# The last two token blocks of a decoder trunk, multiplied jointly by seven products instead of eight

## The chip, the cores and the metric

The kernel runs on one core of one Trainium2 chip. The metric is the device time of one execution in microseconds (us); a profiled execution also has a span, from its first to its last instruction. Engines: PE (TensorE, matmuls), DVE (VectorE), ACT (ScalarE), POOL (GpSimd), SP (SyncE, which issues the DMA transfers). SBUF is the on-chip memory, PSUM the memory that matmuls write (eight banks of 128 x 512 fp32).

## The reference

One layer over 2048 tokens of width 1024, in fp32:

```
h <- x + concat[ SSD(384) | RG-LRU(256) | FoX attention(384) ]( rms(x) W_in ) W_out
h <- h + ( silu(u W_gate) * (u W_up) ) W_down          u = rms(h) * g2, inner width 2816
h <- h + sigmoid( rms(h)*g3 W_pg + b ) * ( p W_pp )    p has width 256
out = rms(h) * gf
```

FoX is causal attention of 6 heads x 64, swept over queries. `W_out` and `W_pg` are 1024 x 1024.

## The kernel before

All activations lie transposed: 128 features on the partitions, tokens along the free axis. The tokens are cut into four blocks of 512 (`TB`, `NTB`), the width into 8 tiles of 128 (`KD`), the inner width into 22 (`NF`).

Every fp32 number is kept as two fp32r numbers, a rounded one and the rest. A weight block (128 output columns, 8 input tiles) comes by DMA into a staging tile (`wst`, 2 buffers), ACT writes its rounded half (L179) and POOL the rest (L180) into a tile `w` (3 buffers); that is `weight`. `parts` and `split` do the same for activations with ACT and DVE into the tiles `u0` to `u7` (2 buffers each). `mm3` (L190 to L192) then makes three matmuls of 128 x 128 by 128 x 512 for each input tile: high x high, high x low, low x high, 24 for a full output tile, into one of three PSUM banks `mm`. Five more banks (`xa` to `xe`) serve the rest.

The program has three phases, each with its own tile pools. Phase 1 projects and runs the RG-LRU; phase 1b runs the convolutions and the SSD and, beside them, attention of query chunk 0. Phase 3 (`phase3`) loops over the four token blocks `tb`: gate and up products in three groups of inner tiles (`FSPLIT`), each followed by its part of the down product added into `h`; then the norm g3, `W_pp`, `W_pg` and the final norm with the output. Attention of chunk `tb + 1` is a generator that runs beside the feed-forward part: `mm3` advances it by `rate / KD` pieces for each input tile (`Side.tick`), with `rate` = its number of pieces over `RATE`. `load_y` then reads back the heads' outputs (`dy`) of the next block, and `mix` makes its `W_out` product beside `W_pg`, so that the next block can start at once. Block 3 has neither attention nor a next block.

`rms` turns a sum of squares (`square_sum`, tiles `ssq` with 1 buffer and `sq` with 3) into reciprocal roots along the tokens: eight small matmuls (L135), a power on POOL (L139), and two matmuls that spread it over the partitions (L149).

The order on each engine is not the order of the code: the tile framework's scheduler lists instructions by readiness and by their place in the program, fixes each engine's queue when the program is built, hands out buffers and adds the semaphores. Each engine then executes its own queue in order.

Of the kernel before, what the change touches and what calls it, by code (L numbers as in the profile page):

```python
# [2 lines left out]

# [1 line left out]

# [6 lines left out]
F32 = mybir.dt.float32  # L12
F32R = mybir.dt.float32r
ACT = mybir.ActivationFunctionType
ALU = mybir.AluOpType
# [16 lines left out]
RATE = 45  # L32


PC = {}
# [29 lines left out]
class Trunk:  # L65
# [589 lines left out]
    def phase3(self, ctx):  # L655
        nc, tc, a = self.nc, self.tc, self.a
        pool = lambda name, bufs, **kw: ctx.enter_context(tc.tile_pool(name=name, bufs=bufs, **kw))
        one = pool("m4one", 1)
        two = pool("m4two", 2)
        V = nc.vector  # L660
        hbp = self.t(one, [P, 8], "hbp")
        nc.vector.tensor_scalar(hbp, self.pc("bple", 0, 8), 0.5, None, op0=ALU.mult)
        side = self.side

        h, u = self.first
        for tb in range(NTB):
            tsl = slice(tb * TB, (tb + 1) * TB)
            more = tb + 1 < NTB
            rate = 0
            if more:  # L670
                side.start(self.attention(tb + 1, one, ("xa", "xe", "xb", "xc"), "xd"))

                rate = 6 * (8 * (tb + 2) + 1) / RATE
            for f0, f1 in zip(FSPLIT[:-1], FSPLIT[1:]):
                hid = []
                for f in range(f0, f1):
                    pg = self.mm3(self.weight(a["w_gate"][f], KD), u, rate)
                    pu = self.mm3(self.weight(a["w_up"][f], KD), u, rate)
                    th = self.t(two, [P, TB], "th")
                    nc.scalar.activation(th, pg, ACT.Tanh, scale=0.5)  # L680
                    nc.vector.scalar_tensor_tensor(th, th, 1.0, pg, op0=ALU.add, op1=ALU.mult)  # L681
                    nc.vector.tensor_tensor(th, th, pu, op=ALU.mult)  # L682
                    hh = self.u(f - f0)
                    nc.scalar.activation(hh[:, 0], th, ACT.Copy, scale=0.5)  # L684
                    nc.vector.scalar_tensor_tensor(hh[:, 1], th, 0.5, hh[:, 0].bitcast(F32), op0=ALU.mult, op1=ALU.subtract)  # L685
                    hid.append(hh)
                if f1 == NF and more:
                    yx = self.load_y(tb + 1)
                for c in range(KD):
                    ps = self.mm3(self.weight(a["w_down"][c, :, f0:f1], f1 - f0), hid, rate)  # L690
                    nc.vector.tensor_tensor(h[c], h[c], ps, op=ALU.add)  # L691
            u = self.norm_split(h, "g3", eng=V, tag="xe")

            px = self.t(one, [P, 4, TB], "kx", F32R)
            px = [px[:, 0:2], px[:, 2:4]]
            for k in range(2):
                y = self.load(a["pt"][k, :, tsl])
# [12 lines left out]
            hn = []  # L710
            for c in range(KD):
                while more and len(hn) < min(c + 4, KD):
                    hn.append(self.mix(tb + 1, len(hn), yx))
# [6 lines left out]
                nc.vector.scalar_tensor_tensor(em[c], th, 0.5, h[c], op0=ALU.mult, op1=ALU.add)  # L720
            if more:
                h, u = hn, un
            rb = self.rms(self.square_sum(em, V), D, "xb")
            for k in range(KD):
                nc.vector.scalar_tensor_tensor(em[k], em[k], self.pc("gf", k), rb, op0=ALU.mult, op1=ALU.mult)
                nc.sync.dma_start(self.out[k, :, tsl], em[k])

    def build(self, phases=3):
        tc, nc = self.tc, self.nc
        with ExitStack() as ctx:  # L730
            pool = lambda name, bufs, **kw: ctx.enter_context(tc.tile_pool(name=name, bufs=bufs, **kw))
            self.cpool = pool("const", 1)
            self.small = pool("small", 2)
            self.tmp = pool("tmp", 2)
            self.dpool = pool("scratch", 1, space=DRAM)
            self.wst, self.wsp = pool("wst", 2), pool("w", 3)
            self.upool = pool("u", 2)
            self.pmm, self.px = pool("pmm", 3, space=PSUM), pool("px", 1, space=PSUM)
            for nm, shape in (("dq", [3, P, 2, T]), ("dk", [3, P, 2, T]), ("dv", [T // P, P, 6 * P]), ("dy", [KD, P, T]),
                              ("du", [NTB, KD, P, TB]), ("ddt", [NTB, P, 2, NCH, 6]),  # L740
                              ("drow", [NTB, NCH * 12, P]), ("dcum", [6, T])):
                setattr(self, nm, self.t(self.dpool, shape, nm))
            self.consts()
            for i, ph in enumerate((self.phase1, self.phase1b, self.phase3)):
                if i == 1:
                    self.hp = pool("h", KD + 3)
                if i < phases:
                    with ExitStack() as c2:
                        ph(c2)
# [50 lines left out]

# [10 lines left out]
```

## Time and profile before

| | us |
|---|---|
| median of 3 runs | 2932.22 (2927.58 to 2932.3) |
| the profiled execution, device time | 2928.33 |
| its span | 2926.6 |
| PE busy | 2812.5 |
| DVE busy | 1751.9 |
| POOL busy | 1213.2 |
| ACT busy | 1175.7 |

Busy time of PE counts pipelined matmuls whose ends are modelled: one of 128 x 512 shows as about 396 ns, while a new one starts every 0.23 us. In a row of groups the columns are line, engine, operation, output tile <- input tiles, shapes, count, then busy us and mean ns of one, then the engine's idle time just before them and what ended it. A row of stretches has start:end, length, and for each engine the busy time with the number of instructions, the granted clock, the share of DMA time and GB/s. A row of the timeline has start, duration, engine (q: issue only), line, operation, tiles, shapes, how many were merged, and in brackets the idle time before and what ended it. A row of one line's instructions has the shortest, median and longest duration in ns.

### The profile page before, as it was taken

The numbers are of one execution on the slowest core, as the hardware profiler recorded it, in microseconds if no ns is written. First come the engines' busy times: TensorE is split into PE (matmuls) and PEld (weight loads), VectorE is DVE, ScalarE is ACT, GpSimd is POOL, SyncE is SP. The second block draws the span as 40 slices with busy tenths as digits, with TensorE's granted clock in tenths as the row PEclk, the third lists the DMA queues.
The fourth block names the chain that finished last, engine by engine and source line by source line (L and its number), as shares of the span: only waits on it lengthen the run. The fifth ranks groups of instructions, "written<-read, shape, count | busy, mean of one in ns | idle before, by whom it ended". The sixth has DMA issues, their size and how long they took to land.

```text
span 2926.6 us, 35034 instructions
## 1 busy us (share of the span) xinstructions
PE 2812.5 (96%) x12981; PEld 2317.3 (79%) x12981; DVE 1751.9 (60%) x3001; ACT 1175.7 (40%) x1751; POOL 1213.2 (41%) x635
## 2 busy tenths in 40 slices
PE   6998999998999999999999999999999999999997
PEld 5777777777888888887888888788888887888885
DVE  7888768988754543637655446464665464523246
ACT  5555434444333332434444334344444343322233
POOL 5544445432443434443333334443333344444442
PEclk9999999998999999999999999999999999999998
DMA  5544544452354343434343334243443233332231
GB/s 181 172 164 159 162 142 141 132 162 80 136 157 131 119 122 104 142 123 133 118 147 104 127 105 146 100 146 115 133 122 114 91 130 108 116 97 92 100 100 65
DMA packets 156221, 368.60 MB, mean 126 GB/s; under 512 B 17644, under 2 KB 49036, under 8 KB 154508
## 3 DMA queue, kind: packets, MB, share of 16 engines
q1 hardware_dynamic: 156050, 366.36, 38.6%
q8 instruction: 103, 1.69, 0.2%
q14 instruction: 68, 0.56, 0.1%
HBM read 322.01 MB, written 44.29 MB: 125 GB/s over the span
## 4 chain that ended last, share of the span: by engine, by line
PE 72%; DVE 3%; issue 1%; DMA 1%; ACT 1%; POOL 0%; POOLq 0%; DVEq 0%; ACTq 0%
PE mm L191 20%; PE mm L192 20%; PE mm L190 20%; PE xd L609 2%; PE xd L608 2%; PE xa L603 1%; DMA ld<-dy 1%; PE xe L603 1%; PE xb L603 1%; PE xc L603 1%; PE xa L572 0%; PE xa L573 0%; DVE th L719 0%; DVE u L168 0%; PE xb L573 0%
## 5 line engine op out<-in xcount | busy, mean ns | idle before, releaser
L180 POOL TENSOR_TENSOR w<-wst,w 128x1024 fp32r<-128x1024 f32 (+1 forms) x424 | 1031.8, 2435 | 1365.6 <-ACT w L179 1300.5
L190 PE MATMUL mm<-u,w 128*128 128x512 f32 x3264 | 1295.9, 399 | 16.5 <-ACT u L200 8.9
L191 PE MATMUL mm<-u,w 128*128 128x512 f32 x3264 | 1289.6, 396 | 13.5 <-DVE u L201 13.5
L192 PE MATMUL mm<-u,w 128*128 128x512 f32 x3264 | 1289.9, 396 | 0.5 <-POOL w L180 0.5
L190 PEld LDWEIGHTS mm<-u,w 128*128 128x128 f32 x3264 | 619.1, 190 | 144.3 <-ACT u L200 10.8
L191 PEld LDWEIGHTS mm<-u,w 128*128 128x128 f32 x3264 | 619.0, 190 | 140.9 <-DVE u L201 17.9
L192 PEld LDWEIGHTS mm<-u,w 128*128 128x128 f32 x3264 | 618.6, 190 | 128.3 <-POOL w L180 0.9
L179 ACT ACTIVATE w<-wst 128x1024 fp32r<-128x1024 f32 (+1 forms) x424 | 440.5, 1040 | 525.1 <-PE mm L192 383.1
L685 DVE SCALAR_TENSOR_TENSOR u<-th,u 128x512 fp32r<-128x512 f32 x88 | 190.6, 2166 | 62.8 <-ACT u L684 62.7
L584 ACT ACTIVATE lg<-lg,m 128x128 f32<-128x128 f32 (+7 forms) x96 | 115.5, 1203 | 155.9 <-DVE m L582 150.9
L161 DVE TENSOR_TENSOR ssq<-ssq,sq 128x512 f32<-128x512 f32 x111 | 134.6, 1212 | 58.0 <-ACT sq L157 55.8
L682 DVE TENSOR_TENSOR th<-th,mm 128x512 f32<-128x512 f32 x88 | 60.4, 686 | 168.0 <-PE mm L192 167.3
L691 DVE TENSOR_TENSOR h<-h,mm 128x512 f32<-128x512 f32 x96 | 65.6, 686 | 127.1 <-PE mm L192 126.7
L680 ACT ACTIVATE th<-mm 128x512 f32<-128x512 f32 x88 | 52.6, 597 | 214.0 <-PE mm L192 213.7
L681 DVE SCALAR_TENSOR_TENSOR th<-th,mm 128x512 f32<-128x512 f32 x88 | 60.3, 685 | 113.1 <-ACT th L680 112.9
L564 POOL TENSOR_TENSOR cd<-cum,maskT 128x128 f32<-128x128 f32 x96 | 47.9, 499 | 182.3 <-DVE mx L577 92.3
L719 DVE SCALAR_TENSOR_TENSOR th<-th,lg 128x512 f32<-128x512 f32 x32 | 31.0, 968 | 111.5 <-ACT th L718 111.4
L587 DVE TENSOR_SCALAR lg<-lg,r 128x128 f32<-128x128 f32 (+7 forms) x96 | 93.6, 975 | 2.6
L609 PE MATMUL xd<-ph,vc 128*128 128x512 f32 x216 | 83.5, 390 | 0.0
L608 PE MATMUL xd<-ph,vc 128*128 128x512 f32 x216 | 80.8, 374 | 0.0
L607 DVE TENSOR_TENSOR ph<-xc,ph 128x512 fp32r<-128x512 f32 (+1 forms) x66 | 36.7, 556 | 48.4 <-ACT ph L606 48.4
L139 POOL TENSOR_TENSOR rr<-rv,mhalf 128x4 f32<-128x4 f32 x28 | 29.1, 1041 | 88.1 <-DVE rv L137 75.3
(293 smaller groups left out, 3212.2 us busy)
## 6 DMA issues: line engine op xcount, KB each, us to landing
wst<-in_w_gate SPq DMA_DIRECT2D x88, 512.0 KB, 3.5
wst<-in_w_up SPq DMA_DIRECT2D x88, 512.0 KB, 3.5
wst<-in_w_down SPq DMA_DIRECT2D x64, 448.0 KB, 3.3
wst<-in_w_out SPq DMA_DIRECT2D x32, 512.0 KB, 3.5
wst<-in_w_down SPq DMA_DIRECT2D x32, 512.0 KB, 3.5
wst<-in_w_pg SPq DMA_DIRECT2D x32, 512.0 KB, 3.5
vc<-dv SPq DMA_DIRECT2D x60, 256.0 KB, 3.8
wst<-in_w_xbc SPq DMA_DIRECT2D x28, 512.0 KB, 4.5
```

The source lines that it names most:

```text
L161: (eng or nc.gpsimd).tensor_tensor(acc, acc, s, op=ALU.add)
L179: nc.scalar.activation(w[:, 0], st, ACT.Copy)
L180: nc.gpsimd.tensor_tensor(w[:, 1], st, w[:, 0].bitcast(F32), op=ALU.subtract)
L190: nc.tensor.matmul(ps, lhsT=w[:, 0, k], rhs=x[:, 0], start=k == 0, stop=False)
L191: nc.tensor.matmul(ps, lhsT=w[:, 0, k], rhs=x[:, 1], start=False, stop=False)
L192: nc.tensor.matmul(ps, lhsT=w[:, 1, k], rhs=x[:, 0], start=False, stop=k == n - 1)
L584: nc.scalar.activation(lg, lg, ACT.Exp, bias=m, scale=1.0, accum_out=l)
L587: nc.vector.tensor_scalar(lg, lg, r, None, op0=ALU.mult)
L603: nc.tensor.transpose(pt[:, qi * P:(qi + 1) * P], probs[qi][:, kt * P:(kt + 1) * P], self.ident)
L608: nc.tensor.matmul(po[:, sl], lhsT=vc[:, kt], rhs=ph[:, 0, sl], start=kt == 0, stop=False)
L609: nc.tensor.matmul(po[:, sl], lhsT=vc[:, kt], rhs=ph[:, 1, sl], start=False, stop=kt == nkt - 1)
L685: nc.vector.scalar_tensor_tensor(hh[:, 1], th, 0.5, hh[:, 0].bitcast(F32), op0=ALU.mult, op1=ALU.subtract)
```

## The change

Phase 3 keeps blocks 0 and 1 only. Block 0 now runs attention of chunks 1 and 2 one behind the other beside its feed-forward part, block 1 attention of chunk 3, with `RATE` 52 instead of 45; the generator is run to its end (`side.finish`) before the last down product.

A new phase (`phase4`, with its own pool `m5`) takes blocks 2 and 3 together through `W_out`, feed-forward part, `W_pg` and output. Each product is a 2 x 2 block product: the two token blocks (i) by even and odd input tiles, and even and odd input tiles by two neighbouring output tiles (c). The Strassen-Winograd scheme makes it from seven half-depth products:

- `moving` makes the seven combinations of activations S1 to S7 in place of `h`, each split in two parts (28 tiles: 16 in the `u` tiles, 12 in `m5`), after which `h` is loaded again from DRAM;
- `stationary` makes seven weight combinations from two staged weight blocks, in place on POOL, split into three `w` tiles and one `wx`;
- `seven` runs the products, accumulates three pairs of them in PSUM, and hands the four results to a function `put`;
- the gated hidden values are combined once (`store`), written to DRAM (`dhid`), and loaded and split by `hidden` in three groups for the down product; `dh` keeps `h`, `dem` the `W_pp` product.

```diff
-        for tb in range(NTB):
+        for tb in range(2):
...
-                side.start(self.attention(tb + 1, one, ("xa", "xe", "xb", "xc"), "xd"))
-                rate = 6 * (8 * (tb + 2) + 1) / RATE
+            more = tb == 0
+            att = (1, 2) if more else (3,)
+            side.start(chain(*(self.attention(q, one, ("xa", "xe", "xb", "xc"), "xd") for q in att)))
+            rate = sum(6 * (8 * (q + 1) + 1) for q in att) / RATE
...
+    def finish_parts(self, t, src, eng):
+        self.nc.scalar.activation(t[:, 0], src, ACT.Copy)
+        eng.tensor_tensor(t[:, 1], src, t[:, 0].bitcast(F32), op=ALU.subtract)
+
+    def moving(self, x, un):
...
+        for p in R:
+            un(2 * p, 0)
+            self.finish_parts(a11[p], x[0][2 * p], V)
+        for p in R:
+            un(2 * p + 1, 1)
+            self.finish_parts(a22[p], x[1][2 * p + 1], V)
+        for p in R:
+            un(2 * p, 1)
+            G.tensor_tensor(x[1][2 * p + 1], x[1][2 * p], x[1][2 * p + 1], op=ALU.add)
+            self.finish_parts(s1[p], x[1][2 * p + 1], V)
+        for p in R:
+            G.tensor_tensor(x[1][2 * p], x[0][2 * p], x[1][2 * p], op=ALU.subtract)
+            V.tensor_tensor(x[0][2 * p], x[1][2 * p + 1], x[0][2 * p], op=ALU.subtract)
+            self.finish_parts(s2[p], x[0][2 * p], V)
+        for p in R:
+            un(2 * p + 1, 0)
+            G.tensor_tensor(x[0][2 * p], x[0][2 * p + 1], x[0][2 * p], op=ALU.subtract)
+            self.finish_parts(s4[p], x[0][2 * p], V)
+        for p in R:
+            self.finish_parts(a12[p], x[0][2 * p + 1], V)
+        for p in R:
+            self.finish_parts(s3[p], x[1][2 * p], V)
+
+    def stationary(self, src, j, k0, k1):
...
+        for c in (2 * j, 2 * j + 1):
+            self.nst += 1
+            pool, tag = ((self.wst, "wst"), (self.m5, "wst2"))[(self.nst // 2) % 2]
+            st = self.t(pool, [P, KD, P], tag, bufs=2)[:, :nk]
+            nc.sync.dma_start(st, src[c, :, k0:k1])
+            r.append(st)
+        b11, b21, b12, b22 = r[0][:, 0::2], r[0][:, 1::2], r[1][:, 0::2], r[1][:, 1::2]
+        W = []
+        for _ in range(3):
+            w = self.t(self.wsp, [P, 2, KD, P], "w", F32R)
+            W += [w[:, 0], w[:, 1]]
+        W.append(self.t(self.m5, [P, KD, P], "wx", F32R))
...
+        self.finish_parts(W[0], b11, G)
+        G.tensor_tensor(b11, b12, b11, op=ALU.subtract)
+        self.finish_parts(W[4], b22, G)
+        self.finish_parts(W[5], b21, G)
+        G.tensor_tensor(b12, b22, b12, op=ALU.subtract)
+        G.tensor_tensor(b22, b22, b11, op=ALU.subtract)
+        G.tensor_tensor(b21, b21, b22, op=ALU.subtract)
+        self.finish_parts(W[1], b21, G)
+        self.finish_parts(W[2], b11, G)
+        self.finish_parts(W[3], b22, G)
+        self.finish_parts(W[6], b12, G)
+
+    def seven(self, W, S, put):
+        A = self.ps(next(self.banks))
+        self.product(A, W[0], S[0], True)
+        s1 = self.t(m5, [P, TB], "s1", bufs=2)
+        nc.scalar.activation(s1, A, ACT.Copy)
+        Dd = self.ps(next(self.banks))
+        self.product(Dd, W[1], S[1], True)
+        C = self.ps(next(self.banks))
+        self.product(C, W[2], S[2], True)
+        s5 = self.t(m5, [P, TB], "s5")
+        nc.scalar.activation(s5, C, ACT.Copy)
+        B = self.ps(next(self.banks))
+        self.product(B, W[3], S[3], True)
+        t6 = self.t(m5, [P, TB], "t6")
+        V.tensor_tensor(t6, s1, B, op=ALU.add)
+        self.product(C, W[4], S[4], False)
+        put(0, 1, t6, C)
+        self.product(A, W[5], S[5], False)
+        put(0, 0, None, A)
+        self.product(B, W[6], S[6], False)
+        t7 = self.t(m5, [P, TB], "t7")
+        V.tensor_tensor(t7, s1, B, op=ALU.add)
+        put(1, 0, t7, Dd)
+        put(1, 1, t7, s5)
...
+    def phase4(self, ctx):
+        self.m5 = m5 = ctx.enter_context(tc.tile_pool(name="m5", bufs=1))
+        self.banks = cycle(("mm", "mm", "mm", "xa", "xb", "xc", "xd"))
...
+        S = self.moving(h, gain_y)
+        refill(lambda k, i: a["xt"][k, :, tsl[i]])
+        for j in range(4):
+            self.seven(self.stationary(a["w_out"], j, 0, KD), S, add(j, True))
...
+        S = self.moving(h, normed("g2"))
+        refill(lambda k, i: self.dh[i, k])
...
+        for j in range(NF // 2):
+            self.seven(self.stationary(a["w_gate"], j, 0, KD), S, put_gate)
+            self.seven(self.stationary(a["w_up"], j, 0, KD), S, put_up(j))
+            store(j)
+        for f0 in range(0, NF, KD):
+            f1 = min(NF, f0 + KD)
+            S = self.hidden(f0 // 2, (f1 - f0) // 2)
+            for j in range(4):
+                self.seven(self.stationary(a["w_down"], j, f0, f1), S, add(j, f1 == NF))
+        S = self.moving(h, normed("g3"))
+        refill(lambda k, i: self.dh[i, k])
...
+        for j in range(4):
+            self.seven(self.stationary(a["w_pg"], j, 0, KD), S, put_pg(j))
+        for i in range(2):
+            rb = self.rms(self.square_sum(h[i], V), D, "xe")
...
```

`product` makes the three matmuls of each of the (four or three) half-depth input tiles. `add` adds a result into `h` on DVE; `put_gate`, `put_up` and `put_pg` first add their two terms on DVE (for the last of the four on POOL: `total`), then apply tanh on ACT and multiply on DVE. `store` makes four sums on POOL and seven transfers. `normed` makes the two blocks' reciprocal roots in bank `xe`, copied to SBUF by ACT. The DMA scratch of the program is set to 1024 bytes, which leaves more SBUF to the tiles.

More of the change, by code (lines that the diff above doesn't have):

```diff
@@ L1 @@
 from contextlib import ExitStack
-from itertools import cycle
+from itertools import chain, cycle
 import numpy as np
@@ L31 @@
 MASK = -1e30
-RATE = 45
+RATE = 52
 PC = {}
@@ L688, in phase3 @@
                     yx = self.load_y(tb + 1)
+                if f1 == NF:
+                    side.finish()
                 for c in range(KD):
@@ L726, in phase3, with slots @@
                 nc.sync.dma_start(self.out[k, :, tsl], em[k])
-    def build(self, phases=3):
+    def slots(self, n):
+        out = []
+        for f in range(7):
+            row = []
+            for p in range(n):
+                j = 4 * f + p
+                row.append(self.u(j % 8) if j < 16 else self.t(self.m5, [P, 2, TB], f"v{j - 16}", F32R))
+            out.append(row)
+        return out
+    def finish_parts(self, t, src, eng):
+        self.nc.scalar.activation(t[:, 0], src, ACT.Copy)
+        eng.tensor_tensor(t[:, 1], src, t[:, 0].bitcast(F32), op=ALU.subtract)
@@ new lines, in moving @@
+    def moving(self, x, un):
+        nc = self.nc
+        V, G = nc.vector, nc.gpsimd
+        S = self.slots(4)
+        a11, a22, s1, s2, s4, a12, s3 = S
+        R = range(4)
+        for p in R:
[20 more added lines that the diff above has]
+            self.finish_parts(s3[p], x[1][2 * p], V)
+        return S
@@ new lines, in hidden @@
+    def hidden(self, j0, n):
+        S = self.slots(n)
+        for f in range(7):
+            for p in range(n):
+                raw = S[f][p][:, 1].bitcast(F32)
+                self.nc.sync.dma_start(raw, self.dhid[j0 + p, f])
+                self.finish_parts(S[f][p], raw, self.nc.vector)
+        return S
+    def stationary(self, src, j, k0, k1):
+        nc = self.nc
+        G = nc.gpsimd
+        nk = k1 - k0
+        r = []
+        for c in (2 * j, 2 * j + 1):
[10 more added lines that the diff above has]
+        W.append(self.t(self.m5, [P, KD, P], "wx", F32R))
+        W = [w.rearrange("p (s k) c -> p s k c", s=2)[:, :, :nk // 2] for w in W]
+        self.finish_parts(W[0], b11, G)
[9 more added lines that the diff above has]
+        self.finish_parts(W[6], b12, G)
+        return W
@@ new lines, in product @@
+    def product(self, ps, W, S, first):
+        nc = self.nc
+        n = len(S)
+        for p in range(n):
+            for q, (a, b) in enumerate(((0, 0), (0, 1), (1, 0))):
+                nc.tensor.matmul(ps, lhsT=W[:, a, p], rhs=S[p][:, b], start=first and p == 0 and q == 0, stop=p == n - 1 and q == 2,
+                                 skip_group_check=not first)
+    def seven(self, W, S, put):
+        nc = self.nc
+        V = nc.vector
+        m5 = self.m5
+        A = self.ps(next(self.banks))
[21 more added lines that the diff above has]
+        put(1, 1, t7, s5)
@@ L729, in build @@
+    def build(self):
         tc, nc = self.tc, self.nc
@@ L802 @@
     arrays = layout(inputs)
-    nc = bacc.Bacc("TRN2", target_bir_lowering=False, num_devices=1)
+    nc = bacc.Bacc("TRN2", target_bir_lowering=False, num_devices=1, dynamic_dma_scratch_size=1024)
     aps = {n: nc.dram_tensor("in_" + n, v.shape, F32, kind="ExternalInput").ap() for n, v in arrays.items()}
```

122 lines of the change are left out of this document (114 added, 8 removed).

## Prediction

> **What bounds the kernel now.** I read the page first (engines, chain), then the sums by stretches, then the groups of instructions, then the timeline at three places.
>
> ```profile
> span 2926.6 us, 35034 instructions
> PE 2812.5 (96%) x12981; PEld 2317.3 (79%) x12981; DVE 1751.9 (60%) x3001; ACT 1175.7 (40%) x1751; POOL 1213.2 (41%) x635
> PE 72%; DVE 3%; issue 1%; DMA 1%; ACT 1%; POOL 0%; POOLq 0%; DVEq 0%; ACTq 0%
> ```
>
> PE is busy 96% of the span and carries the chain that ended last; POOL does not appear in it. Fewer matmuls is therefore the right currency. The stretches are the four blocks of the third phase, the tail after the last matmul, a quiet stretch of the last block, and one short stretch used further down:
>
> ```profile
> core 0: us, PE busy (x) PEld busy (x) DVE busy (x) ACT busy (x) POOL busy (x), PEclk, DMA share, GB/s
> 2347.80:2351.20 3.40, 3.40 (x9) 2.72 (x10) 0.29 (x2) 1.15 (x2) 3.40 (x3) 0.51 0.32 90
> 2600.00:2700.00 100.00, 100.00 (x443) 82.85 (x442) 29.14 (x25) 25.82 (x32) 42.23 (x18) 1.00 0.29 97
> 2908.00:2926.60 18.60, 3.36 (x11) 2.35 (x10) 9.13 (x16) 1.32 (x2) 1.01 (x1) 0.58 0.31 113
> 785.00:1327.50 542.50, 540.13 (x2485) 445.08 (x2483) 274.15 (x468) 207.07 (x307) 229.23 (x119) 1.00 0.41 129
> 1327.50:1889.00 561.50, 556.73 (x2598) 459.47 (x2598) 311.40 (x543) 227.94 (x325) 222.19 (x116) 1.00 0.39 125
> 1889.00:2483.00 594.00, 588.56 (x2780) 485.96 (x2780) 340.21 (x611) 253.45 (x351) 222.94 (x113) 1.00 0.37 118
> 2483.00:2908.00 425.00, 420.35 (x1841) 346.49 (x1841) 175.16 (x173) 128.96 (x169) 178.90 (x77) 0.99 0.28 94
> ```
>
> 443 matmuls in 100 us give 0.2257 us for one. In that quiet stretch POOL is busy 42%, DVE 29%: the spare room that the change spends.
>
> **The budget.** Blocks 1 and 2 (counted from 0) each hold 2016 matmuls of the projections, 455.0 us at 0.2257, so 106.5 and 139.0 us of them are attention and block overhead. The last block has no attention: 425.0 + 18.6 less 1824 matmuls (411.7) leaves 31.9, of which 18.6 is the tail, so 13.3 is overhead of a block's own. Attention of chunk 2 thus costs 93.2 us and of chunk 3 125.7 us; both move into blocks 0 and 1. The new stage begins at 785 + (542.5 + 93.2) + (443.6 + 125.7) = 1990.0 us, and breaks even if it lasts 936.6 us. (RATE 52 puts 252/52 = 4.85 attention pieces beside each group of 24 matmuls, against 198/45 = 4.40 in block 2 now, where DVE is at 57%. I cost that at nothing; the cover is PE's own queue. Scaled, DVE comes to 63%; between 3 us less, as block 1 gets only 3.81, and 6 us more.)
>
> **Matmuls of the stage.** A call of `seven` has 7 products of 12 matmuls (9 in the last group of `w_down`): 4 calls for `w_out`, 22 for gate and up, 12 for `w_down`, 4 for `w_pg`, and 96 plain matmuls of `w_pp`: 3540, against 4032 now. The 492 saved are worth 111.0 us; the stage needs 799.0 us of PE, 18.96 us a call. So 137.6 us may be lost elsewhere before the gain is gone.
>
> **The weight side.** Now a pair of output columns for two blocks takes 4 POOL splits of 1024; `stationary` takes 11 operations of 512 on POOL.
>
> ```profile
> L180 POOL TENSOR_TENSOR w<-wst,w 128x1024 fp32r<-128x1024 f32 (+1 forms) x424 | 1031.8, 2435 | 1365.6 <-ACT w L179 1300.5
> L685 DVE SCALAR_TENSOR_TENSOR u<-th,u 128x512 fp32r<-128x512 f32 x88 | 190.6, 2166 | 62.8 <-ACT u L684 62.7
> L682 DVE TENSOR_TENSOR th<-th,mm 128x512 f32<-128x512 f32 x88 | 60.4, 686 | 168.0 <-PE mm L192 167.3
> ```
>
> L682 (one operand from PSUM) takes 0.69 us; L685, as large but with both operands in SBUF, 2.17 on average: such a DVE operation waits for a running POOL operation. The timeline gives the price on both sides:
>
> ```profile
> 236.40 8.48 DVE L201 TENSOR_TENSOR u<-x,u 128x512 fp32r<-128x512 f32 x5
> 239.24 5.10 POOL L201 TENSOR_TENSOR u<-ld,u 128x512 fp32r<-128x512 f32 x3
> 403.17 3.76 POOL L201 TENSOR_TENSOR u<-ld,u 128x512 fp32r<-128x512 f32 x3
> ```
>
> Three POOL operations alone take 3.76 us, 1.25 each; taking turns with DVE operations 5.10, 1.70 each. So a two-SBUF-operand DVE operation costs a saturated POOL 0.45 us, and a POOL operation costs a saturated DVE about 1.70 - 0.69 = 1.0.
>
> A gate or up call: 11 POOL operations, 1 in `total`, 2 as half of `store`: 14 x 1.25 + 3 DVE (the `put` products) x 0.45 = 18.85 us of POOL, against 18.96 of PE. Both at 99%: no slack. And POOL can't run ahead: the `w` tag has 3 buffers, each holding two of the seven weights, `wx` one, so W4 and W5 of the next call wait for the sixth product of this one, and b22, b21 and then W1 (overwritten in place) wait behind them. That is 5 POOL operations and 2 ACT copies, 5 x 1.25 + 2 x 0.6 = 7.4 us, against 5.4 us until PE wants W1 in the written order. The order can heal this (products 2 and 5 before 1). ACT, in one queue, waits too: a copy into a buffer not yet free holds up the `s1` and tanh copies that free PSUM. Loss per call: from 0 (all healed; PE's own work excludes less) to 6.0 (rival 3). I take 1.5, nearer the healed end because POOL's throughput just suffices: 33 us. For the other 20 calls POOL needs 11 x 1.25 + 4 x 0.45 = 15.6 us; 0 to 2.2, I take 0.8: 16 us.
>
> The Trainium skill (SBUF — State Buffer, "Who interferes with whom") states that whichever of the two engines issues first has the shared pair for the whole instruction and the other fully blocks. By it a turn is 1.25 + 0.69 = 1.94 and a gate or up call at least 14 x 1.25 + 3 x 0.69 = 19.6 us, so no order could lose less than 13 us over the 22 calls and rival 1 would end at 2916. The trace's 1.70 for a turn is lower, and I go by the trace.
>
> **The boundary and the start.** Tiles of a new phase wait for the old phase's tiles:
>
> ```profile
> 812.92 1.88 DVE L222 TENSOR_TENSOR sq<-ys,xa 128x512 f32<-128x512 f32 x3 [3.81 <-PE xa L149]
> 814.84 2.38 DVE L662 TENSOR_SCALAR hbp<-par 128x8 f32<-128x8 f32 x1
> 814.88 0.60 ACT L680 ACTIVATE th<-mm 128x512 f32<-128x512 f32 x1 [0.17 <-DVE sq L222]
> 815.25 0.50 SPq L554 DMA_DIRECT2D qx<-dq  x1
> 2907.80 0.39 PE L192 MATMUL mm<-u,w 128*128 128x512 f32 x1
> 2912.14 1.86 PE L135 MATMUL xb<-ones,ssq 128*128 128x1 f32 x8 [3.95 <-DVE ssq L161]
> 2917.78 5.36 DVE L725 SCALAR_TENSOR_TENSOR lg<-lg,par,xb 128x512 f32<-128x512 f32 x8 [0.89 <-PE xb L149]
> 2918.55 4.94 SPq L726 DMA_DIRECT2D out_t<-lg  x8
> ld<-dy SPq DMA_DIRECT2D x32, 256.0 KB, 3.5
> L200 ACT ACTIVATE u<-sq x64: 612/630/635, 786.4 to 2868.8; 128x512 fp32r<-128x512 f32 x64
> ```
>
> The third phase's first tiles (hbp, th, qx) are all written within half a us after the second's last read (L222, ended 814.80). So m5's tiles, `h0` among them, wait for the third phase's tail, and that tail of 18.6 us (already in 443.6) becomes a hole in PE. After it: load 3.5, gain 0.7, ACT copy 0.63, DVE 0.69: first product after 5.5 us. Then `moving` must feed 7 products: 34 two-SBUF-operand DVE operations still to do x 0.69 + 20 POOL operations x 1.0 = 44 us, while PE has the first call's products and, by buffers and banks, some 3 of the second: 9.5 x 2.71 = 26. Loss 5.5 + 44 - 26, less what overlaps: **20** (12 to 35).
>
> **The normalisations inside the stage.** w_out to g2: after PE's last product 3 adds, 9 square sums, 4 `dg`, 16 gains, 4 differences, 28 splits: 64 DVE operations x 0.69 = 44, plus 18 POOL x 1.0 = 18, partly in the wait for the reciprocal root (L135 to L725: 5.6 us, twice, since both use bank `xe`): last product fed about 60 us after; PE does 10 products (27 us) and one more. Loss **32** (20 to 45). w_down to g3: the same plus 4 for its own splits, less 96 `w_pp` matmuls (21.7 us) as cover: **14** (5 to 25). The three `hidden` loads: slots come free product by product, 28 splits with some 13 POOL operations, 33 us, begin 13 us before the group does: 3.7 each, **11** (0 to 25).
>
> **Transfers.**
>
> ```profile
> GB/s 181 172 164 159 162 142 141 132 162 80 136 157 131 119 122 104 142 123 133 118 147 104 127 105 146 100 146 115 133 122 114 91 130 108 116 97 92 100 100 65
> L626 SPq DMA_DIRECT2D ld<-dy x32: 319/326/787, 515.2 to 2341.6; - x32
> ```
>
> A `hidden` group loads 7.3 MB; the busiest slice of the page has 181 GB/s, so 7.3 MB lasts at most 40 us, against 33 of splits. I cost it at nothing; with the cover gone 7 us a group. Some 280 loads and stores of activations are added, 84 weight loads and 32 others go: 170 more issues pass SP, 0.33 us each, 56 us of some 950. A store waiting for POOL stands ahead of the next weight load, which has one call (19 us) of slack through the doubled raw buffers.
>
> **The end.** Two blocks finish together: 18.6 plus a second root (5.6) and a second set of products (5.4): **29** (26 to 32).
>
> **Sum.** 799.0 + 33 + 16 + 20 + 32 + 14 + 11 + 29 = 954.0; end at 2944.0, 17.4 over the span. The profiled execution took 2928.33 for a span of 2926.6, and the median of the runs, 2932.22, is 3.9 over that: **2950 us**, 0.6% slower.
>
> **Rivals.**
> 1. *The scheduler fills it all* (faster). Place: the calls' steady state. If products are ordered by readiness, POOL's 18.85 fits under 18.96 and only 2 us of the 49 remain: stage 907, time 2903; with smaller holes down to 2880. For: in the last block PE overtakes the wait for splits well:
>
> ```profile
> 2858.39 2.06 DVE L211 SCALAR_TENSOR_TENSOR sq<-h,par,xe 128x512 f32<-128x512 f32 x3 [1.13 <-PE xe L149]
> 2868.69 1.48 DVE L201 TENSOR_TENSOR u<-sq,u 128x512 fp32r<-128x512 f32 x2
> ```
>
> there 16 DVE operations lasted 11.8 us (2858.39 to 2870.17) and block overhead stayed at 13.3. Against: that block has three whole weight buffers and a POOL at 42%. It decides if the mean loss over the 42 calls is under 0.75 us.
> 2. *A draw*: the holes as forecast and 0.6 to 0.9 us lost a call, 2926 to 2938.
> 3. *PE keeps the written order.* Then W4 to W1 to product 1 to product 5 is a loop: 7.4 + 5 x 2.71 = 21.0 us a call, and with `total` and `store` ahead in POOL's queue 22.2 and 27.2; the mean 24.7, 5.8 over PE, x 22 = 127, and 2.0 x 20 = 40 for the rest: stage 1072, time 3067. Against: the scheduler reorders; for: its order is fixed by its own durations, and one DVE instruction (L720 below) varies from 0.68 to 2.77 us with POOL beside it. A stall may cost more than itself:
>
> ```profile
> 2345.11 0.39 PE L191 MATMUL mm<-u,w 128*128 128x512 f32 x1
> 2346.88 1.08 PE L135 MATMUL xd<-ones,ssq 128*128 128x1 f32 x8 [1.38 <-DVE ssq L161]
> L720 DVE SCALAR_TENSOR_TENSOR lg<-th,h x32: 677/692/2774, 1264.0 to 2909.7; 128x512 f32<-128x512 f32 x32
> ```
>
> After the 1.4 us of idleness before L135 the clock stood at 0.51 for 3.4 us (2347.8 to 2351.2), 1.7 us lost. The Trainium skill (TensorE: Matmul & The Clock Gate, "Why this matters for your kernels") asks only that idle gaps stay under some 3 us between bursts; by that such stalls would cost nothing more, which this row contradicts. With the row's price on every call rival 3 would reach 3067 + 42 x 1.7 = 3138.
>
> **How the numbers follow.** Chances: forecast 0.37 (its own range 2938 to 2995), rival 1 0.35, rival 2 0.11, rival 3 0.17. A difference under 0.2%, some 6 us, can't be told from none. Faster 0.35, same 0.11, slower 0.54. The range takes in rival 1's lower holes and reaches to rival 3: 2885 to 3065, with about 1 in 10 left out on each side.
>
> **What would show it.** Right: POOL busy over 85% through gate and up; the stage's first matmul some 24 us after block 1's last; two stretches of about 60 us with PE at half; blocks 0 and 1 ending near 1421 and 1990. Wrong: calls 19.0 us apart throughout (rival 1), 22 to 27 us apart with PE waiting on POOL at product 1 (rival 3), `h0` written before the last output store (boundary), or attention stretching block 0 past 650 us.

## The result, and the profile after

The changed kernel takes 3081.36 us (median of 4 runs, 3078.33 to 3082.84) against 2929.9 us of the kernel before beside it: a ratio of 1.0516 [1.0498, 1.0534]. The forecast was 2950 us, in a range of 2885 to 3065: the sign is right, the size is not. The profiled execution took 3078.33 us, with a span of 3076.5 us where the sum gave 2944.0. The 132.5 us between them are the question.

The page of the changed kernel, its engines, two rows of its slices, and the group that `finish_parts` makes of the weights:

```profile
span 3076.5 us, 35435 instructions
PE 2769.4 (90%) x12489; PEld 2244.0 (73%) x12489; DVE 1991.7 (65%) x3267; ACT 1273.8 (41%) x2046; POOL 1630.4 (53%) x1035
PE   6998899999999999989999999767799989888765
PEclk9999999998999999999999999878899999999887
L743 POOL TENSOR_TENSOR w<-wst,w 128x512 fp32r<-128x512 f32 (+1 forms) x252 | 357.4, 1431 | 123.2 <-ACT w L742 117.5
```

492 matmuls fewer (12981 to 12489), as counted, but PE's busy time fell by 43 us only, and its share from 96% to 90%: many matmuls of the stage ran at a lower granted clock (0.69 to 0.94 in five of the rows below, 0.55 in the tail). The dips are where the slices of PE fall to 6 and 7 and stay at 8. The same stage by stretches (from one call's last sum `t7`, which ends a call, to another's): the `w_out` calls; to the end of gate0; 20 gate and up calls; up10; five rows with the twelve `w_down` calls; to the end of pg0, with `w_pp`; pg1 to pg3; the tail. Columns as before.

```profile
2003.90:2118.20 114.30, 88.46 (x348) 66.46 (x348) 81.49 (x88) 47.54 (x82) 90.27 (x60) 0.87 0.39 134
2118.20:2189.80 71.60, 38.62 (x111) 25.00 (x112) 61.35 (x73) 27.69 (x48) 39.84 (x25) 0.69 0.21 67
2189.80:2608.90 419.10, 398.85 (x1681) 319.66 (x1680) 158.03 (x164) 131.18 (x222) 378.46 (x280) 0.98 0.28 97
2608.90:2642.40 33.50, 26.42 (x107) 20.68 (x107) 32.34 (x29) 22.41 (x41) 27.12 (x17) 0.90 0.79 267
2642.40:2701.40 59.00, 53.17 (x228) 42.06 (x227) 35.02 (x35) 15.10 (x26) 50.56 (x35) 1.00 0.24 76
2701.40:2730.70 29.30, 26.07 (x109) 20.86 (x107) 28.84 (x26) 19.10 (x36) 22.86 (x15) 0.94 0.83 287
2730.70:2790.90 60.20, 55.62 (x231) 43.90 (x230) 33.82 (x39) 16.98 (x30) 45.28 (x31) 0.97 0.16 49
2790.90:2821.40 30.50, 26.16 (x110) 20.12 (x110) 27.77 (x27) 18.48 (x34) 21.62 (x16) 1.00 0.61 206
2821.40:2881.90 60.50, 55.95 (x232) 44.04 (x232) 41.84 (x50) 22.76 (x40) 46.12 (x37) 0.97 0.34 112
2881.90:2979.30 97.40, 52.95 (x206) 41.99 (x205) 68.70 (x80) 42.95 (x75) 51.99 (x33) 0.75 0.42 146
2979.30:3036.70 57.40, 56.45 (x244) 45.14 (x242) 38.59 (x37) 21.61 (x36) 46.81 (x31) 1.00 0.20 71
3036.70:3076.50 39.80, 6.34 (x20) 4.70 (x20) 27.70 (x46) 9.50 (x16) 3.29 (x3) 0.55 0.30 106
```

Take 18.96 us of PE's work a call (14.2 in the last group of `w_down`) from each stretch, and what is left is its loss. The forecast column includes the 1.5 or 0.8 us a call of the sum:

| | measured | forecast | miss |
|---|---|---|---|
| stage starts at 2003.9 | | 1990.0 | 13.9 |
| `w_out` calls and start, 114.3 - 75.8 | 38.5 | 23.2 | 15.3 |
| to gate0, 71.6 - 19.0 | 52.6 | 33.5 | 19.1 |
| 20 gate and up calls, 419.1 - 379.2 | 39.9 | 30.0 | 9.9 |
| up10 and `w_down`, 273.0 - 227.5 | 45.5 | 22.1 | 23.4 |
| to pg0, 97.4 - 19.0 - 21.7 | 56.7 | 14.8 | 41.9 |
| pg1 to pg3, 57.4 - 56.9 | 0.5 | 2.4 | -1.9 |
| tail | 39.8 | 29.0 | 10.8 |

The steady calls are the smallest positive miss. The holes around them were too small in the forecast, all of them, and the one that was to be filled with `w_pp` most.

Two waits make most of the hole at pg0. The timeline of PE, ACT and DVE there:

```profile
2908.21 1.83 PE L135 MATMUL xe<-ones,ssq 128*128 128x1 f32 x8 [15.69 <-DVE ssq L161]
2913.04 2.77 PE L987 MATMUL xc<-wst,w 128*128 128x512 f32 x6
2961.39 1.22 PE L824 MATMUL xa<-u,w 128*128 128x512 f32 x2 [22.06 <-ACT w L742]
2908.16 0.60 ACT L989 ACTIVATE sq<-xc 128x512 f32<-128x512 f32 x1 [6.05 <-DVE ssq L161]
2901.96 2.49 DVE L743 TENSOR_TENSOR u<-h,u 128x512 fp32r<-128x512 f32 x4
2907.38 0.68 DVE L161 TENSOR_TENSOR ssq<-ssq,sq 128x512 f32<-128x512 f32 x1
```

L987 is `w_pp`'s matmul and L989 its evacuation, the copy of a finished bank into SBUF. PE did nothing for 15.69 us although 54 of `w_pp`'s 96 matmuls were still to come. Its first seven output tiles had filled the seven banks; the evacuation that frees a bank writes into tiles `sq`, these held squares of block 3, and DVE added those squares only between and behind block 2's splits (L743), up to 2908.06. So the cover waited for the work that it was to cover. The second wait, 22.06 us, is for a weight of the third product that pg0 ran.

### The profile page after: what moved, and what is told of

The parts are those of the page before. It is cut to its first block, busy times and chain, and to the rows that moved or that the text cites. A ratio compares the mean times of both kernels' runs of the same rounds, so it can differ in the third digit from the quotient of the medians.

```text
span 3076.5 us, 35435 instructions
## 1 busy us (share of the span) xinstructions
PE 2769.4 (90%) x12489; PEld 2244.0 (73%) x12489; DVE 1991.7 (65%) x3267; ACT 1273.8 (41%) x2046; POOL 1630.4 (53%) x1035
## 5 line engine op out<-in xcount | busy, mean ns | idle before, releaser
L180 POOL TENSOR_TENSOR w<-wst,w 128x1024 fp32r<-128x1024 f32 (+1 forms) x256 | 632.4, 2472 | 817.5 <-ACT w L179 782.0
L190 PE MATMUL mm<-u,w 128*128 128x512 f32 x1952 | 782.0, 402 | 11.3 <-ACT u L200 5.3
L191 PE MATMUL mm<-u,w 128*128 128x512 f32 x1952 | 779.0, 400 | 10.3 <-DVE u L201 10.3
L192 PE MATMUL mm<-u,w 128*128 128x512 f32 x1952 | 777.9, 399 | 4.7 <-POOL w L180 4.7
L190 PEld LDWEIGHTS mm<-u,w 128*128 128x128 f32 x1952 | 371.8, 191 | 88.6 <-ACT u L200 6.3
L191 PEld LDWEIGHTS mm<-u,w 128*128 128x128 f32 x1952 | 371.8, 190 | 86.3 <-DVE u L201 13.8
L192 PEld LDWEIGHTS mm<-u,w 128*128 128x128 f32 x1952 | 371.8, 190 | 81.3 <-POOL w L180 6.0
L743 POOL TENSOR_TENSOR w<-wst,w 128x512 fp32r<-128x512 f32 (+1 forms) x252 | 357.4, 1431 | 123.2 <-ACT w L742 117.5
L179 ACT ACTIVATE w<-wst 128x1024 fp32r<-128x1024 f32 (+1 forms) x256 | 267.0, 1043 | 253.9 <-PE mm L192 118.6
L742 ACT ACTIVATE w<-wst 128x512 fp32r<-128x512 f32 (+1 forms) x252 | 151.4, 617 | 313.3 <-PE mm L824 62.7
L824 PE MATMUL mm<-u,w 128*128 128x512 f32 x870 | 234.5, 415 | 32.1 <-ACT w L742 13.6
L824 PEld LDWEIGHTS mm<-u,w 128*128 128x128 f32 x870 | 173.3, 201 | 78.6 <-DVE u L743 16.7
L824 PE MATMUL mm<-v,w 128*128 128x512 f32 x435 | 111.2, 401 | 8.2 <-ACT s L835 6.8
L824 PE MATMUL xa<-u,w 128*128 128x512 f32 x279 | 77.7, 414 | 35.9 <-ACT w L742 25.7
L684 DVE SCALAR_TENSOR_TENSOR u<-th,u 128x512 fp32r<-128x512 f32 x44 | 90.2, 2051 | 24.2 <-ACT u L683 24.0
L824 PEld LDWEIGHTS mm<-v,w 128*128 128x128 f32 x435 | 82.2, 190 | 30.6 <-ACT s L835 9.2
```

The costliest lines, as they stand in the source:

```text
L179: nc.scalar.activation(w[:, 0], st, ACT.Copy)
L180: nc.gpsimd.tensor_tensor(w[:, 1], st, w[:, 0].bitcast(F32), op=ALU.subtract)
L190: nc.tensor.matmul(ps, lhsT=w[:, 0, k], rhs=x[:, 0], start=k == 0, stop=False)
L191: nc.tensor.matmul(ps, lhsT=w[:, 0, k], rhs=x[:, 1], start=False, stop=False)
L192: nc.tensor.matmul(ps, lhsT=w[:, 1, k], rhs=x[:, 0], start=False, stop=k == n - 1)
L742: self.nc.scalar.activation(t[:, 0], src, ACT.Copy)
```

## The experiments

All times are medians of four runs, beside 3081.36. In diffs `G` is POOL, `V` is DVE. Phase 3's first tile `hbp`, ahead of which no experiment edits anything, starts between 812.83 and 821.18 us in the profiled executions; so totals that lie less than some 8 us apart can't be told apart, and stretches say more than totals.

**1. Weights without combinations.**

```diff
-        G.tensor_tensor(b11, b12, b11, op=ALU.subtract)
-        G.tensor_tensor(b12, b22, b12, op=ALU.subtract)
-        G.tensor_tensor(b22, b22, b11, op=ALU.subtract)
-        G.tensor_tensor(b21, b21, b22, op=ALU.subtract)
```

> Leaves out the four combinations of weight blocks per call (168 POOL operations); their splits, the matmuls and all buffers stay. Theory H (the loss sits in the holes where PE waits for activations: the normalisations, the hidden loads, the start and the tail; POOL limits only the gate and up calls): the 22 gate and up calls give back about 40 us, and the holes some 15 to 45 because POOL has less to do between DVE's turns: 2995 to 3025 us. Theory W (the weight side, POOL's 11 operations a call and the loop of buffers, holds PE back everywhere): 150 us or more comes back, under 2930 us. Under 30 us would mean that POOL's load in the calls is not a cost at all.

2989.80 us, 91.6 less. Stretches to gate0, 20 calls, up10 with `w_down`, to pg0:

```profile
2111.20:2177.70 66.50, 39.41 (x125) 27.30 (x126) 57.20 (x73) 27.78 (x48) 32.03 (x20) 0.72 0.22 78
2177.70:2558.80 381.10, 381.10 (x1662) 311.68 (x1662) 132.70 (x162) 128.50 (x221) 272.12 (x202) 1.00 0.30 105
2558.80:2810.60 251.80, 239.83 (x1023) 194.14 (x1022) 173.94 (x203) 111.95 (x203) 138.48 (x95) 0.97 0.45 154
2810.60:2891.60 81.00, 50.92 (x190) 38.79 (x189) 61.39 (x75) 39.85 (x72) 42.69 (x26) 0.81 0.43 149
```

The 20 calls lose 38.0 us and then PE has no gap at all (381.10 of 381.10); 21.2 come from up10 and `w_down`, 16.4 from pg0, 5.1 from gate0. That is Theory H, 5 us below its range, and far from W: POOL limited the calls, but even with its load lifted the kernel is 2.1% slower than before.

**2. Activations without combinations.** The three `G` lines and the one `V` line of `moving` that combine blocks are dropped.

> Leaves out the combinations of activations in the three uses of moving (12 POOL and 4 DVE operations each); gains, splits and matmuls stay. Theory H: each of the three stretches loses 12 turns of 1.7 us on POOL and 4 operations on DVE, partly beside other work, so 15 to 25 us each: 3005 to 3035 us, with the weight calls as before. Theory W: weights would still come late, 3065 to 3081 us.

3034.59 us, 46.8 less, at the upper end of H. To gate0, then to pg0:

```profile
2112.10:2168.40 56.30, 32.20 (x109) 22.94 (x110) 47.35 (x71) 26.77 (x50) 17.72 (x14) 0.70 0.31 103
2854.80:2940.60 85.80, 56.33 (x206) 43.01 (x205) 51.98 (x75) 41.48 (x75) 34.20 (x21) 0.78 0.47 161
```

15.3 us from gate0 and 11.6 from pg0. From `hbp` of the new pool to the end of out0 it takes 48.4 us instead of 54.9.

**3. A second root of its own.**

```diff
-            rb = self.rms(self.square_sum(blocks, V), n, "xe")
+            rb = self.rms(self.square_sum(blocks, V, i == 1), n, ("xe", "xd")[i])
```

(`square_sum` with `True` uses `q0` to `q3`; the final roots are both made before the final gains.)

> The second token block's reciprocal root gets scratch tiles and a PSUM bank of its own, and both final roots are asked for ahead of the final gains; no work is removed. Theory H: the two roots run one behind the other today (16 us between them at w_out to g2, 15 at the tail), so 10 to 15 us come back at each of the two inner normalisations and about 10 at the tail: 3040 to 3056 us. Theory W: only the tail moves, 3070 to 3077 us.

3059.82 us, 21.5 less: between the two theories, nearer to H. The hole to gate0 went from 71.6 to 63.9 us, to pg0 from 97.4 to 91.8, the tail from 39.8 to 33.6. Serial roots cost 6 to 8 us at each place, not 10 to 15, since block 2's gains and splits run under the second root.

**4. `w_pp` behind `w_out`.** The whole loop is moved ahead of `normed`, and `sq` becomes `q{c % 4}`.

> The 96 matmuls of w_pp with their loads move from behind w_down to behind w_out, and their evacuation uses the tiles q0 to q3, idle there, in place of sq. Theory H: w_pp covers nothing where it stands (its evacuation shares the tiles sq with the square sums, and its weights hold the buffers that w_pg needs): its 21.7 us fill the hole behind w_out, and the hole behind w_down shrinks from 97 to about 70 us with no more matmuls in it: 3037 to 3060 us. Theory W, or if cover is worth the same in either hole: 3075 to 3090 us.

3062.31 us, 19.1 less. To gate0, now with `w_pp`, and to pg0, now without:

```profile
2120.50:2208.00 87.50, 60.19 (x207) 41.88 (x206) 70.80 (x73) 39.92 (x72) 52.74 (x32) 0.80 0.43 142
2886.30:2960.20 73.90, 38.49 (x108) 25.05 (x109) 62.75 (x74) 28.34 (x48) 41.51 (x26) 0.68 0.21 71
```

To pg0: 73.9 - 19.0 leaves 54.9 us of hole without `w_pp`, against 56.7 with it. Had `w_pp` filled a part of the hole, the rest would have been smaller with it; it was 1.8 us larger. The stretch is 23.5 us longer with `w_pp` for 21.7 us of matmuls, so as cover it was worth nothing there. In the other place the stretch grew by 15.9, so 5.8 of the 21.7 were covered. What held it up there is order: the small matmuls of block 2's root (L135) stood in PE's queue behind `w_pp`. They ran 11.65 us after their sum was ready (2119.84), and block 3's first square needs the one tile `ssq` that they read, so it starts 16 us after block 2's last:

```profile
2118.48 0.63 ACT L157 ACTIVATE sq<-h 128x512 f32<-128x512 f32 x1 [1.99 <-DVE h L905]
2119.15 0.69 DVE L161 TENSOR_TENSOR ssq<-ssq,sq 128x512 f32<-128x512 f32 x1 [0.70 <-ACT sq L157]
2131.49 0.95 PE L135 MATMUL xe<-ones,ssq 128*128 128x1 f32 x8
2134.24 0.63 ACT L157 ACTIVATE ssq<-h 128x512 f32<-128x512 f32 x1
```

The move itself brings 7.6 us; 16.9 came from the 20 calls, 402.2 instead of 419.1 us, in which nothing was edited but each engine's queue has another order.

**5. Additions on DVE.** In `total` and `store` each `G.tensor_tensor` becomes `V.tensor_tensor`.

> The additions in total and store that POOL makes in the gate and up calls (6 in each pair of calls) are made by DVE; nothing is left out. Theory P (POOL's count of operations sets the pace of these calls, and DVE, busy 0.37 there, has room): POOL falls from 14 to 11 operations a call, the pairs of calls come 38 us apart and the four up calls of 25 to 27 us go: 3036 to 3051 us. Theory S (both engines take turns, so an operation moved to DVE takes as much of POOL's time as before): 3071 to 3083 us.

3060.53 us, 20.8 less. The 20 calls:

```profile
2195.70:2595.20 399.50, 389.96 (x1679) 315.22 (x1679) 227.99 (x223) 131.86 (x222) 317.74 (x221) 1.00 0.31 101
```

59 operations fewer on POOL took 60.7 us from it (378.46 to 317.74) and cost DVE 70.0; the stretch is 19.6 us shorter, 20.0 a call. Theory S falls, and P's size was too large (the least it allowed was 30 us): three up calls still take 23 to 24 us, with POOL busy 0.69 to 0.79 of them. The Trainium skill (Perfetto Trace Analysis, "Optimizing Scalar/DVE Operations") warns that moving work between these two engines might not help, since they share a port; here it did, by these 20 us.

**6. `moving`'s combinations on DVE.** Its three `G.tensor_tensor` become `V.tensor_tensor`.

> The 12 combinations of activations that POOL makes in each use of moving are made by DVE; nothing is left out. Theory P (in these stretches the path goes through POOL's operations at 1.7 us each, and DVE waits for them): each of the three stretches gets 8 to 12 us shorter: 3041 to 3058 us. Theory D (DVE, busy 0.86 there, is the engine that sets them): 12 more operations of 0.69 us each make each stretch 5 to 8 us longer: 3096 to 3106 us.

3061.53 us, 19.8 less, between the theories but far nearer to P. Yet only pg0 did what P says (97.4 to 86.4); to gate0 it grew from 71.6 to 75.2, and 13.5 us came from the 20 calls. It doesn't settle which engine sets these holes.

**7. Hidden loads without the low half.**

```diff
-                self.finish_parts(S[f][p], raw, self.nc.vector)
+                self.nc.scalar.activation(S[f][p][:, 0], raw, ACT.Copy)
```

> Leaves out DVE's 77 subtractions that make the low halves in the three hidden loads (the low half stays the unsplit value); loads, ACT copies and matmuls stay. Theory H (the splits, taking turns with POOL's weight operations, set the stretches at up10, dn0.3 and dn1.3, which lose some 45 us over PE's work): 20 to 35 us come back: 3046 to 3061 us. Rival (the tiles come free too late, or the loads from DRAM set it): 3070 to 3083 us.

3052.84 us, 28.5 less. The three stretches with loads:

```profile
2609.90:2631.60 21.70, 21.15 (x92) 17.00 (x91) 8.00 (x9) 16.90 (x31) 17.75 (x14) 1.00 0.94 320
2691.10:2710.10 19.00, 19.00 (x84) 15.57 (x83) 8.62 (x9) 11.22 (x21) 11.21 (x9) 1.00 0.89 302
2771.60:2793.40 21.80, 19.79 (x86) 15.88 (x85) 8.58 (x9) 14.15 (x26) 12.96 (x11) 1.00 0.79 264
```

33.5, 29.3 and 30.5 us became 21.7, 19.0 and 21.8: 30.8 us in all is what DVE's splits cost. DVE had been busy for 88.95 of the 93.3 us, and without them for 25.20 of 62.5.

**8. Three edits together**, `w_pp` at the start of the stage. Experiment 5, experiment 3 (for D = 1024 only), and the loop of `w_pp` ahead of `rf`.

> Three edits together, nothing left out: the gate and up additions on DVE, the second token block's roots with scratch and a PSUM bank of their own, and w_pp at the very start of the stage, evacuated into q0 to q3. If the savings are separate they add up: 20 for the roots, 35 for the additions, 15 to 40 for w_pp (more if the hole at the start has room for its 21.7 us): 2985 to 3012 us, still above the kernel before. If the holes only move, 3030 us or more.

3052.56 us, 28.8 less: it did not add up. `w_pp` at the start made out0 end 34.1 us later, at 2092.9 (6.2 of them stood already at block 1's last matmul, as many as at the start of phase 3), for 21.7 us of matmuls; the stretch to pg0 got 31.5 shorter, of which experiments 4 and 3 account for 23.5 and 5.6.

**9. No roots at g2 and g3.**

```diff
-            rb = [rstd(h[i], i, D) for i in range(2)]
-            return lambda k, i: V.scalar_tensor_tensor(..., rb[i], ...)
+            return lambda k, i: V.scalar_tensor_tensor(..., h[i][k], ...)
```

> Leaves out the square sums and reciprocal roots at the norms g2 and g3 of the new stage (each gain takes h itself in place of the root, so its duration stays). Theory R (the two roots, one behind the other, are the larger part of these two holes): the stretch to gate0 falls from 72 to 45 to 52 us and the one to pg0 from 97 to 70 to 80: 3026 to 3041 us. Theory D (the gains, splits and combinations on DVE and POOL fill the time anyway, and a root mostly runs beside them): 8 to 14 us a hole: 3053 to 3065 us.

3037.12 us, 44.2 less: Theory R by the total. The work starts earlier, in the call before, so two calls are compared: from out2 to gate0 67.3 instead of 90.9 us, from dn2.1 to pg0 110.4 instead of 127.9. Square sums and roots are worth 23.6 and 17.5 us.

**10. Four edits together**, `w_pp` in its place: experiments 3, 5 and 6, and `q{c % 4}` for `sq` in `w_pp`.

> Four edits together, nothing left out: the roots of the second block on scratch and a bank of their own, the gate and up additions on DVE, moving's combinations on DVE, and w_pp left in its place but evacuated into q0 to q3. The first three saved 21, 20 and 20 us alone. If separate: 3005 to 3025 us. If holes only move into each other, as three other edits together did: 3035 us or more. Neither reaches the kernel before.

3025.74 us, 55.6 less, where the three alone had come to 62.1: nearly separate, and the least that any version with the whole computation took, still 1.0334 [1.0307, 1.036] of the kernel before. The stretch to pg0 takes 92.1 us, as in experiment 3 (91.8), although it also holds experiment 6's edit, which alone took 11.0 off it: tiles of its own for `w_pp`'s evacuation show no gain in this company. The wait of 15.69 us is gone, but PE waits 9.5 and 8.7 us for weights and 9.4 for a root there. What these tiles would do alone was not run.

**11. Block 1 without its final norm.**

```diff
-            rb = self.rms(self.square_sum(em, V), D, "xb")
+            if more:
+                rb = self.rms(self.square_sum(em, V), D, "xb")
```

(and the gains under the same condition.)

> Leaves out the final norm of block 1 (its square sum, root and gains); the output is stored without it. Theory B (every tile of the new stage's pool waits for the old phase's last instruction): the boundary moves 12 to 16 us towards block 1's last matmul, and the time with it: 3064 to 3070 us. Rival (loads, gains and splits set the first product anyway): 3076 to 3083 us.

3059.34 us, 22.0 less, 5 us below Theory B's range. The first tile of the new stage's pool, in the changed kernel and in this one:

```profile
2003.94 0.17 DVE L867 TENSOR_SCALAR hbp<-par 128x8 f32<-128x8 f32 x1 [2.98 <-DMA out_t<-lg]
```

```profile
1987.34 0.17 DVE L869 TENSOR_SCALAR hbp<-par 128x8 f32<-128x8 f32 x1 [3.25 <-DMA h<-dy]
```

16.6 us earlier: the boundary follows the tail. 6.0 us of that were there at block 1's last matmul already (1985.65 to 1979.65), because a wait of block 1 is gone (the last one under "A term put at nothing" below). So the boundary itself moved by 10.6 us, a little less than the 12 to 16 expected.

**12. Thinner attention.** `RATE = 60`.

> RATE 60 in place of 52: attention of the first two blocks is spread thinner over the same matmuls (4.2 pieces beside each group of 24 in block 0 rather than 4.85), nothing is left out. Forecast had block 0 end at 1420.7 and block 1's matmuls at 1971.4; they ended some 7 and 14 us later. Theory A (attention is too dense beside the matmuls, and DVE's share there costs PE): both blocks get 3 to 7 us shorter each: 3068 to 3077 us. Theory N (the time goes elsewhere: the norm inside block 0, and weights of the new stage made early beside block 1's end): within 3 us of the changed kernel's 3081, or longer if the thinner spread leaves attention for the down products.

3087.80 us, 6.4 more. Block 1's last matmul ends 6.9 us later (1992.50), but 4.2 of these were there at the start of phase 3 already (819.01 against 814.84), so blocks 0 and 1 got 2.7 us longer, not 6 to 14 shorter: Theory A falls.

**13. First weights ahead of `moving`**, with `w_pp` as in experiment 4.

```diff
+        W = self.stationary(a["w_pg"], 0, 0, KD)
         S = self.moving(h, normed("g3"))
```

(and the same for `w_out` and `w_gate`.)

> The kernel with w_pp behind w_out (3062.3 us), and the first call's weights of w_out, gate and w_pg stand ahead of moving in the program; nothing is left out. Theory Q (the weight operations of the first call queue behind moving's on POOL, and PE waits for W1): the three stretches get 4 to 8 us shorter each: 3040 to 3052 us. Rival (the activations' own chain of root, gain, combination and split ends last): 3057 to 3068 us.

3063.74 us, 1.4 more than experiment 4, which can't be told from none: to gate0 88.2, to pg0 75.6. Theory Q falls for this arrangement. It says nothing of the 22.06 us that the changed kernel waits for a weight: neither this kernel nor experiment 4 has a long wait for weights left to pg0, and PE waits for the root and the splits instead (what waits for what, total us, times, longest):

```profile
PE xe L149 <- DVE sq L147: 11.8, 3, 8.0
PE mm L824 <- DVE u L743: 10.1, 5, 4.4
```

**14. Everything but the old place of `w_pp`.** Experiments 13, 5 and 6, and 3 with `s5` and `s1` for scratch.

> The same, with three edits more: the gate and up additions and moving's combinations on DVE, and the second block's roots on scratch tiles (s5, s1) and a bank of their own; nothing is left out. Alone these saved 20, 20 and 21 us; together with w_pp left behind w_down they came to 3025.7. If Theory Q holds and the savings stay separate: 2985 to 3005 us. If the holes only change their cause: 3010 to 3030 us. In no theory does it reach the kernel before.

3032.73 us, above both expected ranges and 7.0 more than experiment 10, which is too little to rank the two. To gate0 it takes 89.3 us, to pg0 73.4: the holes keep the size that they have in experiment 4 (87.5 and 73.9) and change their cause. To pg0 PE now waits 12.2 us for a root and 8.3 for a weight.

## Why the prediction was wrong

**Right.** That it came out slower, as forecast, is in part luck: the forecast stood 17 us above the kernel before, and every hole was larger than it said. The boundary: block 1's last matmul ended at 1985.65 and the stage's first started at 2009.69, 24.0 us later, as said, and experiment 11 shows what it hangs on. Two long stretches had PE at half (38.62 of 71.6 us, 52.95 of 97.4). POOL was busy 90% through gate and up. The steady calls lost 2.0 us, forecast 1.5; neither rival 1 (19.0 us apart) nor rival 3 (22 to 27) is what the trace shows, for a call took 20.95 on average. Rival 3's time, 3067, was nearly met by another road.

**The step that failed first: `w_pp` "as cover"** (23.5 of the 41.9 us at pg0). The sum took its 21.7 us of matmuls off the hole. They filled nothing of it: without `w_pp` the stretch is 23.5 us shorter (experiment 4). Work covers a hole only if it runs without the engines that make the hole, and `w_pp` has 4 splits on DVE, 4 large ones on POOL and 16 evacuations on ACT, in line with the squares. Experiments 4 and 8 put it in two other places and it cost 15.9 and about 28 us there. Tiles of its own for the evacuation showed no gain in the old place (experiment 10).

**The second, and the larger: the normalisations' terms were sums of DVE time** (19.1 us at gate0, and the other 18.4 at pg0, where the hole without `w_pp` is 54.9 us and the sum without its cover would have had 14 + 21.7 + 0.8 = 36.5; 37.5 us in all). The sum had the last product to gate0 fed about 60 us after the stretch begins; the last split ended 73.6 us after (2118.2 to 2191.84). DVE was busy for 61.35 us of the stretch, much as forecast (44 + 18 = 62), but around that stand waits in the roots, of which the sum took only a part. Against it were set "10 products and one more" of PE, 30 us, four of them in the second call. That head start was not kept: at the last split PE had run 14 of the second call's matmuls, little more than one product. The granted clock in that stretch was 0.69, so PE also went slowly through what it had. What the roots, combinations and weight operations are worth there, taken out one at a time: 23.6, 15.3 and 5.1 us; for pg0 17.5, 11.6 and 16.4. Each was measured alone, so they need not add up.

**The third: the three hidden loads, "11 (0 to 25)"**, counted 33 us of splits a group with most of it beside the group before. Experiment 7 gives 30.8 for the three. That is above the range: DVE was nearly full, as forecast, but what wasn't hidden beside the group before was 10 us a group, not 3.7. The transfer was rightly costed at nothing: without the splits the first of these stretches ran at 320 GB/s for 21.7 us, 6.9 MB, with PE busy for 21.15 of them, where I had taken 181 GB/s for the most.

**Smaller.** The start: 15.3 over. The first product came 5.8 us after the first tile, for 5.5 forecast, so the excess lies in feeding the first call. PE's longest wait there, 8.15 us, is for the second root of the heads' norm, which the term for the start doesn't price; but with tiles of its own for that root (experiment 3) the call ended no sooner, so what sets it stays open. The tail: 39.8 for 29; experiment 3 gives 6.2 of the 10.8, the second root behind the first's gains. The steady calls: 9.9 over; three up calls of 26 to 27 us (up0, up1, up8) make most of it. Experiments 1 and 5 show that POOL's load sets the pace, but experiments 4 and 6 shortened these calls without touching them, by the order alone; which wait decides there stays open.

**A term put at nothing: blocks 0 and 1** (13.9 us, before the stage starts). The sum costed the denser attention there at nothing. Its density is indeed not what cost (experiment 12). Two waits at the end of block 0 and one near the end of block 1 have together the size of the miss; they show on PE, the last beside the POOL operation that held it up:

```profile
1315.69 1.30 PE L149 MATMUL xd<-sq,ones 128*128 128x512 f32 x2 [4.58 <-DVE sq L147]
1323.66 1.65 PE L190 MATMUL mm<-kx,w 128*128 128x512 f32 x3 [6.66 <-ACT kx L699]
1974.29 1.65 POOL L760 TENSOR_TENSOR h<-h,h 128x512 f32<-128x512 f32 x1 [7.46 <-DVE u L743]
1978.74 0.68 PE L192 MATMUL mm<-u,w 128*128 128x512 f32 x1 [3.61 <-POOL w L180]
1979.22 0.63 PE L190 MATMUL mm<-u,w 128*128 128x512 f32 x1
1982.20 0.45 PE L191 MATMUL mm<-u,w 128*128 128x512 f32 x1
```

The first two, for the root in `load_y` and for `w_pp`'s operand, are in the trace of every changed version; in block 0 of the kernel before PE waits at most 1.3 us at a time. There attention ended at 1108.1 us and this root's small matmuls ran among the large ones (1193.7); now attention lasts until 1303.8, and they follow at 1310.17 with the down products over. The code gives the likely reason: `load_y` runs the generator to its end before it asks for this root, and block 0's generator now holds chunk 2 as well, whose result block 1 doesn't need yet. No run took chunk 2 out of the way. The third is the new stage itself: its first combinations (L760) stand in POOL's queue ahead of block 1's weights, and one of them waits 7.46 us for a split. In experiments 2, 6, 10 and 14, where POOL makes no combinations of activations, this wait is missing and blocks 0 and 1 take 5.8 to 6.4 us less (in experiment 11 too, 5.5 us, by another order).

**Open.** Which chain sets the start of the stage, and which wait decides the steady calls.

## What to carry to other kernels

Price a hole by its chain, from the last product to the first, with each wait in it, and count only what another engine brings to it unaided: matmuls whose operands and evacuations run through the engines of the chain were no cover here, and in PE's own queue they can stand ahead of the chain's next step. Look at the seam as well: the new stage's first operations can stand in a queue ahead of the old stage's last ones. Do not credit a head start to the next stretch unless its own limit would let it run ahead. And when a fix takes away one wait, look for the next one: here four edits were nearly additive, but two of them with a third in another place were not.

## What the runs showed of the hardware

The granted clock was the surprise. Before, it was 0.984 on average, after it 0.953, and in the holes 0.69, 0.75 and 0.55. After the 3.61 us of idleness above, matmuls started some 0.43 us apart until 1982.20, and 0.23 only then: 3.46 us at half speed, so 1.7 us on top of the wait. The Trainium skill (TensorE: Matmul & The Clock Gate, "What's actually happening") puts the busy time after which the full clock comes back at about 3.4 us, and the row agrees. It is not always so: in experiment 12 the same wait was followed by 5.7 us at that pace (1984.50 to 1990.22). The hole to gate0 shows it among short waits, where 11 matmuls take 5.06 us and the next 12 take 3.07:

```profile
2137.42 5.06 PE L824 MATMUL mm<-u,w 128*128 128x512 f32 x11 [4.08 <-DVE u L743]
2143.17 3.07 PE L824 MATMUL mm<-v,w 128*128 128x512 f32 x12 [0.69 <-ACT s L835]
```

All 111 matmuls of that stretch took 38.62 us of busy time, 0.35 each, against 0.24 in the 20 calls. So part of what PE did in the holes it did at about half speed, and no term of the sum had that.
